# Two decoder layers on one core: the mean square behind three norms from three sums, taken ahead of the residual's update; order of the matmuls in some k-tiles

## The chip, the core and the metric

One core of a Trainium2 chip runs the whole program. The metric is the time of one execution on the device in microseconds (us); of three executions of the kernel before, the median is 2229.39 us.

## What is computed

The reference is two consecutive layers of a hybrid decoder trunk, 256 tokens of width 2048, all in float32. With shift, scale and gate rows from a projection of silu(c):

```
h  = RMSNorm(x) * (1 + scale_a) + shift_a
y  = concat(mLSTM(h @ W_in), attention(h @ W_in)) @ W_out
x  = x + gate_a * RMSNorm(y)
h' = RMSNorm(x) * (1 + scale_m) + shift_m
x  = x + gate_m * RMSNorm(relu(h' @ W_up)^2 @ W_down)
```

W_up is 2048 x 8192, W_down 8192 x 2048. RMSNorm divides by the root of the mean square over the 2048 columns and multiplies by a weight row. What matters here is the seam between two products: y is normed, added to x, and the sum is normed again before it can be multiplied by the next weight.

## The kernel before, in words

**Products.** Each float32 product is made of three products of rounded halves: a weight tile comes from HBM in loads of 1 MB (queue of SyncE, L231, six buffers called `raw`). ScalarE (ACT) copies half a load to the rounded `whi` (`split_hi`, L275), VectorE (DVE) subtracts it to get the rest `wlo` (`split_lo`, L285). Some pieces go into other buffers, with names like `hi_4h` (high half) and `hi_4l` (low half). Activations are split likewise (`hh`, `hl`, halves of a tile `ht`). A `Unit` is 512 output columns over all k-tiles; its matmuls on TensorE (PE) are at L389, or at L409 and L410 for wide units (`body_wide`: one matmul of 512 columns against `whi`, called W here, one of 256 against `wlo`, called n, for each of four column blocks of a k-tile: W n W n W n W n). One split feeds two k-tiles, called a slab. In layer 0 the rows of scale, shift and gate are still being made: `ada_op` (L244) streams 1 MB of weights through DVE, one instruction each.

**Seams.** Where a product ends and a norm leads to the next, `turn` (L587 to L660) writes the order out by hand: out-projection to up-projection of layer 0 (turn 1), down-projection of layer 0 to the in-projection of layer 1 (turn 2), out-projection to up-projection of layer 1 (turn 3). While it does so, every instruction is held in program order on its engine, and its line shows as L63. The 256 tokens are two tiles of 128 (token tile 0 and 1). The last unit of the old product runs token tile 0 first; while PE does token tile 1, ACT and DVE bring tile 0 through:

- `evac`: the square of y with its sum (ACT, `jko`, or `jkd` in turn 2), y times the gate row (DVE, `yg`; in turn 2 `ys`, last chunk `yl`), four chunks of 512 columns; only the last is within the turn, in turn 2 also the third of token tile 1 (`early`);
- `gain`: the four sums to r, one over the root (`rp..`, five small instructions on DVE and one on ACT);
- `update`: x = yg * r + x, four chunks (DVE);
- squares of the new x with their sums (ACT, `jkm`, or `jka`), then `root` (`rn..`), the same small chain;
- `scale`: x times that root for chunks 0 and 1 (`xn`, one on DVE, one on ACT);
- `group`: four transposes on PE (into `pst`), scale and shift (ACT, `hf`), rounding to `hh` (ACT), the rest `hl` (DVE).

Then the first matmuls of the new unit start with group 0 of tile 0, and tile 1 goes the same way; its group 0 is done by `group_fast`, in which DVE makes `hl` in two halves. The splits of the weights of the new unit (`split_hi`, `split_lo`) stand between these steps at written places. Chunks 2 and 3 follow outside the hand-written order (L62). After layer 1 the last norm updates x and stores it, with no second norm.

In the stages ahead of turns 1 and 3 (the out-projection, units `op_0` to `op_3` of 512 columns), `evac_out` (L1149) empties each unit; ahead of turn 2 `evac_down` (L1274) adds up the down-projection. A scheduler puts these among the splits by its own estimate.

Of the kernel before, what the change touches and what calls it, by code (L numbers as in the profile page):

```python
# [39 lines left out]
def hymba_kernel(ctx: ExitStack, tc: tile.TileContext, x_d, c_d, cols_d, cons_d, wada_d,  # L40
# [248 lines left out]
    def split():  # L289
        split_hi()  # L290
        split_lo()
# [48 lines left out]
    def xdone(n=1):  # L340
        live["x"] -= n
# [56 lines left out]
    def body_ws(u, xh, xl, wh, wl, kt):  # L398
        for j in range(4):
            cs = slice(j * P, (j + 1) * P)  # L400
            u.products(u.ps[j // 2][:, (j % 2) * S:(j % 2) * S + S], j // 2,
                       ((wh[:, cs], xh), (wh[:, cs], xl), (wl[:, cs], xh)), kt)

    def body_wide(u, xh, xl, wh, wl, kt):


        for j in range(4):
            cs = slice(j * P, (j + 1) * P)
            T.matmul(u.ps[j], wh[:, cs], u.act.both(kt), start=kt == 0, stop=False, skip_group_check=True)  # L409
            T.matmul(u.ps[j][:, 0:S], wl[:, cs], xh, start=False, stop=kt == u.nk - 1, skip_group_check=True)  # L410

    def body_mix(u, xh, xl, wh, wl, kt):
        for j in range(2):
# [28 lines left out]
    class PreNorm:  # L442


        def __init__(self, tag, l, vsc, vsh, yg=None, ssy=None):
            self.tag, self.l, self.vsc, self.vsh, self.yg, self.ssy = tag, l, vsc, vsh, yg, ssy
            self.xn, self.groups, self.r = {}, {}, {}

        def gain(self, tok):

# [4 lines left out]
        def update(self, tok, r, sq=None, store=False, between=None):  # L455

            for c in range(4):
                xc = x[:, tok, CH[c]]
                if r is not None:
                    V.scalar_tensor_tensor(xc, self.yg[c][tok], r, xc, ALU.mult, ALU.add)  # L460
                if between is not None and c == 3:
                    V.scalar_tensor_tensor(self.yg[c][tok], xc, 1.0, xc, ALU.mult, ALU.mult, accum_out=sq[:, c:c + 1])
                    between()
                elif sq is not None:
                    square_sum(xc, sq[:, c:c + 1], f"jk{self.tag}_{tok}_{c}")
                if store:
                    nc.sync.dma_start(out_d[tok, :, CH[c]], xc)
# [9 lines left out]
        def scale(self, tok, chunks):  # L477
            for c in chunks:
                o = self.xn[c, tok] = ytile(f"xn{self.tag}_{c}_{tok}")
                if c % 2:  # L480
                    A.activation(o, x[:, tok, CH[c]], AF.Copy, scale=self.r[tok])
                else:
                    V.tensor_scalar(o, x[:, tok, CH[c]], self.r[tok], None, ALU.mult)

        def norm(self, tok):
            sq = self.squares(tok)
            self.update(tok, None, sq)
            self.root(tok, sq)
            self.scale(tok, range(4))

        def group(self, g, tok):

            hh, hl, mods, hf = self.begin(g, tok)
            ps = xalloc(f"pst{self.tag}_{g}_{tok}")
            for k in range(4):
                T.transpose(ps[:, k * P:(k + 1) * P], self.xn[g, tok][:, k * P:(k + 1) * P], ident)
            for k, (gc, sc) in enumerate(mods):
                A.activation(hf[:, k, :], ps[:, k * P:(k + 1) * P], AF.Identity, bias=sc, scale=gc)
            xdone()
            A.activation(hh, hf, AF.Copy)  # L500
            return lambda: V.tensor_tensor(hl, hf, hh.bitcast(F32), ALU.subtract)
# [85 lines left out]
    def turn(units, evac, early, nrm, make, staged=None):  # L587

        s0 = st["mm"]
        units[0].slabs(1)
        split_to(s0 + 7)
        rest = []
        for i, u in enumerate(units[1:]):
            if early is not None and i == 3:
                early(0)
            side()  # L600
            rest.append((u, take()))
            u.mm(rest[-1][1], toks=(0,))
# [17 lines left out]
        units[-1].mm(rest[6][1], toks=(1,))  # L620
# [29 lines left out]
        strict["on"] = False  # L650
        for tok in range(2):
            nrm.scale(tok, range(2, 4))
        if staged:
            order, wide, small, done = staged
            xnT = {g: wide.tile([P, 4, S], F32, tag="sl", name=f"xnT{nrm.tag}_{g}") for g in (2, 3)}
            for tok in range(2):
                nrm.turn_in(xnT, tok, 2)
            strict["last"].clear()
            for m in make[1:]:
                units.append(m())  # L660
                units[-1].slabs(4)
            for e in range(4, 8):
                nrm.modulate(e, xnT, small)
                for u in order:
                    units[u].slabs(1)
                    if e == 7 and u < 3:
                        done(u, units[u])
            return units
        for g in (2, 3):
            for tok in range(2):  # L670
                nrm.group(g, tok)()
# [23 lines left out]
    for l in range(DEPTH):  # L695
# [449 lines left out]
        cT = lambda kt: (cg[kt // 4][0][:, kt % 4, :], cg[kt // 4][1][:, kt % 4, :])  # L1145
        yg = [[None, None] for _ in range(4)]
        ssy = smp.tile([P, 2, 4], F32, tag="ssy", name=f"ssy{L}")

        def evac_out(ps, c, tok):  # L1149
            yg[c][tok] = ytile(f"yg{L}_{c}_{tok}")  # L1150
            square_sum(ps[tok], ssy[:, tok, c:c + 1], f"jko{L}_{c}_{tok}")
            V.tensor_tensor(yg[c][tok], ps[tok], gps[l, GTA][:, CH[c]], ALU.mult)

        def evac_out_task(ps, c):
            for tok in range(2):
# [33 lines left out]
            t.finish()  # L1189


        hT2 = PreNorm("m" + L, l, SCM, SHM, yg, ssy)
        sT_ = {}
        ysum = [[None, None] for _ in range(4)]
        ssm_ = smp.tile([P, 2, 4], F32, tag="ssy", name=f"ssm_{L}")

        def s_tiles(u):
            sT_[u] = [sp.tile([P, 4, S], F32R, tag=f"s{a}", name=f"s{a}{L}_{u}") for a in "hl"]
# [73 lines left out]
        def evac_down(ps, e, c, tok):  # L1272
            if e == 0:
                ysum[c][tok] = ytile(f"ys{L}_{c}_{tok}")  # L1274
                A.activation(ysum[c][tok], ps[tok], AF.Copy)
                return
            yt = ysum[c][tok]
            V.tensor_tensor(yt, yt, ps[tok], ALU.add)
            if e == 7:
                square_sum(yt, ssm_[:, tok, c:c + 1], f"jkd{L}_{c}_{tok}")  # L1280
                o = yt
                if c == 3:
                    o = smp.tile([P, 4, P], F32, tag="hf", bufs=2, name=f"yl{L}_{tok}").rearrange("p a b -> p (a b)")
# [151 lines left out]
```

## Time and profile before

| | |
|---|---|
| times of the runs, us | 2231.54, 2229.39, 2228.36 |
| profiled execution, us | 2228.4 |
| its span in the profile, us | 2226.6 |
| busy share PE, DVE, ACT | 97%, 77%, 49% |
| mean granted TensorE clock | 0.988 |
| turn 1, 2, 3, us of the span | 406 to 440, 1132 to 1168, 1484 to 1519 |

The profiled execution is 1.8 us longer than its span (start and end), and 1.0 us shorter than the median. The profile gives a start and a duration for each instruction; matmuls overlap, so their pitch (from start to start) counts, not the duration. In a timeline row, the bracket is the idle time of the engine ahead of the instruction and what ended it; a row with "x4" is four alike, with one duration for all. The granted clock is the share of full speed that the throttle gave TensorE.

### The profile page before, as it was taken

To read this page: it belongs to the slowest core of one execution; us is meant where nothing else is said; L and a number is where in the kernel's file an instruction comes from. 1 tells how busy PE (TensorE), PEld (TensorE's weight loads), DVE (VectorE), ACT (ScalarE), POOL (GpSimd) and SP (SyncE) were. 2 spreads that over 40 slices of the span, in tenths; PEclk is the share of its full clock that TensorE was granted. 3 is DMA by queue.
4 is the path that set the end of the run, shared out by engine and by line. 5 is a ranking of instruction groups with operands and counts; after the bars stand their busy time and mean duration, and the time that the engine had idled before them with its cause. 6 is when DMAs were issued, how large, how long until landed. Compare 5 with 4: busy or idle time off the path is not lost.

```text
span 2226.6 us, 29814 instructions
## 1 busy us (share of the span) xinstructions
PE 2153.4 (97%) x11658; PEld 1836.8 (82%) x11658; DVE 1710.8 (77%) x2327; ACT 1102.1 (49%) x1597; POOL 1.4 (0%) x15
## 2 busy tenths in 40 slices
PE   6789999899999999999989999999999999999998
PEld 5779777798888888888879988778888888888886
DVE  7989999787888888888667898967566767555556
ACT  4246753645444444434555566556443444444434
POOL 0000000000000000000000000000000000000000
PEclk9999999999999999999999999999999999999999
DMA  9998679597889888888538866755666667655552
GB/s 380 390 366 301 238 301 350 199 355 306 305 318 343 295 337 315 316 319 313 202 131 328 314 229 245 263 191 196 236 223 233 228 225 265 209 189 189 189 189 76
DMA packets 82351, 589.88 MB, mean 265 GB/s; under 512 B 9185, under 2 KB 9633, under 8 KB 10785
## 3 DMA queue, kind: packets, MB, share of 16 engines
q1 hardware_dynamic: 82210, 587.98, 72.0%
q8 instruction: 91, 1.49, 0.3%
q14 instruction: 50, 0.41, 0.1%
HBM read 585.81 MB, written 2.13 MB: 264 GB/s over the span
## 4 chain that ended last, share of the span: by engine, by line
PE 85%; DVE 9%; ACT 3%; issue 2%; DMA 1%; SPq 0%; DVEq 0%; ACTq 0%
PE dn L389 31%; PE up L409 17%; PE up L410 9%; PE op L389 5%; PE up L389 5%; DVE raw L244 4%; PE om L389 3%; PE qa L389 2%; PE qm L389 2%; PE vm L389 2%; DVE wlo L285 2%; PE km L389 2%; PE kva L389 1%; PE up L63 1%; DVE x L63 1%
## 5 line engine op out<-in xcount | busy, mean ns | idle before, releaser
L285 DVE TENSOR_TENSOR wlo<-raw,whi 128x1024 fp32r<-128x1024 f32 x699 | 849.6, 1222 | 409.7 <-ACT whi L275 408.1
L275 ACT ACTIVATE whi<-raw 128x1024 fp32r<-128x1024 f32 x699 | 737.0, 1060 | 842.5 <-PE dn L389 338.7
L409 PE MATMUL up<-htm,whi 128*128 128x512 f32 x1664 | 588.2, 399 | 0.0
L410 PE MATMUL up<-htm,wlo 128*128 128x256 f32 x1664 | 466.9, 281 | 0.0
L244 DVE SCALAR_TENSOR_TENSOR raw<-raw,cact 128x2048 f32<-128x2048 f32 x192 | 437.3, 2284 | 8.2 <-DMA raw<-in_wada_dram 8.1
L389 PE MATMUL dn<-whi,sh 128*128 128x512 f32 x1004 | 391.3, 390 | 0.9 <-DVE r L1224 0.9
L389 PE MATMUL dn<-wlo,sh 128*128 128x512 f32 x1004 | 390.8, 389 | 0.0
L389 PE MATMUL dn<-whi,sl 128*128 128x512 f32 x1004 | 390.7, 389 | 0.0
L409 PEld LDWEIGHTS up<-htm,whi 128*128 128x128 f32 x1664 | 312.6, 188 | 77.6
L410 PEld LDWEIGHTS up<-htm,wlo 128*128 128x128 f32 x1664 | 314.2, 189 | 0.6
L389 PEld LDWEIGHTS dn<-whi,sh 128*128 128x128 f32 x1004 | 188.4, 188 | 41.0 <-DVE r L1224 1.4
L389 PEld LDWEIGHTS dn<-wlo,sh 128*128 128x128 f32 x1004 | 188.4, 188 | 39.6
L389 PEld LDWEIGHTS dn<-whi,sl 128*128 128x128 f32 x1004 | 188.5, 188 | 38.9 <-DVE sl L1246 0.2
L389 PE MATMUL op<-whi,ct 128*128 128x512 f32 x432 | 138.6, 400 | 2.6 <-ACT whi L275 1.8
L389 PEld LDWEIGHTS op<-whi,ct 128*128 128x128 f32 x432 | 81.6, 190 | 21.8 <-ACT whi L275 2.7
L389 PE MATMUL vm<-whi,hta 128*128 128x512 f32 x224 | 77.6, 429 | 21.1 <-ACT whi L275 18.5
L389 PE MATMUL qa<-hta,whi 128*128 128x256 f32 x512 | 93.7, 284 | 0.0
L389 PE MATMUL up<-htm,whi 128*128 128x256 f32 x512 | 93.0, 284 | 0.0
L389 PE MATMUL op<-wlo,ct 128*128 128x512 f32 x216 | 85.3, 401 | 3.0 <-DVE wlo L285 3.0
L389 PE MATMUL om<-whi,hta 128*128 128x512 f32 x256 | 82.2, 401 | 0.0
L389 PEld LDWEIGHTS up<-htm,whi 128*128 128x128 f32 x512 | 80.2, 192 | 0.5
L389 PEld LDWEIGHTS qa<-hta,whi 128*128 128x128 f32 x512 | 80.0, 192 | 0.7 <-issue 0.7
(388 smaller groups left out, 2435.7 us busy)
## 6 DMA issues: line engine op xcount, KB each, us to landing
raw<-in_wada_dram SPq DMA_DIRECT2D x192, 1024.0 KB, 6.3
raw<-in_wdn_dram SPq DMA_DIRECT2D x128, 1024.0 KB, 5.0
raw<-in_wup_dram SPq DMA_DIRECT2D x120, 1024.0 KB, 5.4
raw<-in_win_dram SPq DMA_DIRECT2D x56, 1024.0 KB, 5.3
raw<-in_wout_dram SPq DMA_DIRECT2D x32, 1024.0 KB, 6.6
raw<-in_wst_dram SPq DMA_DIRECT2D x16, 1024.0 KB, 7.6
raw<-in_wsu_dram SPq DMA_DIRECT2D x8, 1024.0 KB, 6.7
gp<-gdr SPq DMA_DIRECT2D x4, 1024.0 KB, 4.9
```

The costliest lines, as they stand in the source:

```text
L63: made = tc.keep_in_program_order(make(*args, **kw))
L244: V.scalar_tensor_tensor(w, w, 1.0, cact, ALU.mult, ALU.mult, accum_out=modc[l][:, v, j:j + 1])
L275: A.activation(hi, raw, AF.Copy)
L285: V.tensor_tensor(lo, raw, hi.bitcast(F32), ALU.subtract)
L389: T.matmul(o, a, w, start=not self.started[b], stop=last and i == 2, skip_group_check=True)
L409: T.matmul(u.ps[j], wh[:, cs], u.act.both(kt), start=kt == 0, stop=False, skip_group_check=True)
L410: T.matmul(u.ps[j][:, 0:S], wl[:, cs], xh, start=False, stop=kt == u.nk - 1, skip_group_check=True)
```

## The change

1. The mean square of the new x is no longer taken from the new x. As x' = x + r*y, sum(x'^2) = sum(x^2) + r * (sum(2xy) + r * sum(y^2)). The new `branch` follows every `yg` (in the out stages and, for the last slabs, the down stage of layer 0): DVE multiplies y, 2 and x with a sum, and writes the products, which nobody reads, over the emptied PSUM tile; ACT squares y with a sum (`jkb`). The new `old` squares the old x on ACT (`jkx`), two chunks with each of the first two `evac` steps of a token tile. `root_after` combines the sums with r in four small DVE instructions and takes the root, so the root comes ahead of the updates. For each of three turns that is eight more DVE instructions of 128x512 with a sum, of which one replaces an old square on DVE, and on ACT eight `jkb` and eight `jkx` in place of seven squares of the new x.
2. The turn then goes chunk by chunk: `step(0)`, `scale(0)`, `step(1)`, `scale(1)`, all on DVE; the steps of chunks 2 and 3 come later. The four parts of `group` are placed one by one.
3. The splits, the evacuation of tile 1 and `hl` stand at other places in the order; the transposes of group 1 of tile 1 go ahead of two runs of matmuls on PE.
4. In `body_wide` every eighth k-tile is ordered W W n n W W n n: 52 k-tiles of 26 units.

The queues of SyncE (all loads) and GpSimd have the same instructions in the same order.

```diff
     def body_wide(u, xh, xl, wh, wl, kt):
-        for j in range(4):
+        for j, wide in ONES if kt % 8 else TWOS:
...
+        def old(self, tok, c):
+            square_sum(x[:, tok, CH[c]], self.sums_of(tok)[:, 0, c:c + 1], f"jkx{self.tag}_{tok}_{c}")
+        def branch(self, tok, c, waste):
+            q, y = self.sums_of(tok), self.yg[c][tok]
+            V.scalar_tensor_tensor(waste, y, 2.0, x[:, tok, CH[c]], ALU.mult, ALU.mult, accum_out=q[:, 1, c:c + 1])
+            square_sum(y, q[:, 2, c:c + 1], f"jkb{self.tag}_{tok}_{c}")
...
+            V.tensor_reduce(q, self.sums[tok], AX.X, ALU.add)
+            V.tensor_scalar(v, q[:, 2:3], r, q[:, 1:2], ALU.mult, ALU.add)
+            V.scalar_tensor_tensor(v, v, r, q[:, 0:1], ALU.mult, ALU.add)
+            V.tensor_scalar(v, v, 0.0, 1.0 / D, ALU.max, ALU.mult)
+            self.r[tok] = rsqrt_one(v, 1, f"rn{self.tag}_{tok}")
...
         evac(0)
         r = nrm.gain(0)
         if not ahead:
             split_hi()
-        sq = nrm.squares(0)
-        nrm.update(0, r, sq)
-        if not ahead:
-            split_lo()
-        nrm.root(0, sq)
-        split_hi()
-        nrm.scale(0, range(2))
-        low = nrm.group(0, 0)
+        nrm.root_after(0, r)
+        nrm.step(0, 0, r)
+        nrm.scale(0, (0,), ())
+        nrm.step(1, 0, r)
+        nrm.scale(0, (1,), ())
+        steps = nrm.group(0, 0)
         units[-1].mm(rest[6][1], toks=(1,))
-        split_lo()
+        for f in steps[:3]:
+            f()
+        nrm.step(2, 0, r)
+        if not ahead:
+            split_lo()
+        split_hi()
         if early is not None:
             early(1)
+        steps[3]()
+        nrm.step(3, 0, r)
+        split_lo()
         evac(1)
-        low()
-        r = nrm.gain(1)
-        low = nrm.group(1, 0)
+        steps = nrm.group(1, 0)
...
-        sq = nrm.squares(1)
-        nrm.update(1, r, sq, between=low)
-        nrm.root(1, sq)
+        r = nrm.gain(1)
+        steps[0]()
+        nrm.root_after(1, r)
+        steps[1]()
+        steps[2]()
+        nrm.step(0, 1, r)
+        nrm.scale(1, (0,), ())
+        nrm.step(1, 1, r)
+        nrm.scale(1, (1,), ())
         split_hi()
-        nrm.scale(1, range(2))
-        nrm.group_fast(0, 1, split_lo)
+        steps[3]()
+        def between():
+            split_lo()
+            nrm.step(2, 1, r)
+        nrm.group_fast(0, 1, between)
         four.append(take())
         unit.mm(four[2], toks=(0,))
+        steps = nrm.group(1, 1)
         unit.mm(four[0], toks=(1,))
-        split()
-        low = nrm.group(1, 1)
         unit.mm(four[1], toks=(1,))
-        low()
+        split_hi()
+        for f in steps:
+            f()
+        split_lo()
+        nrm.step(3, 1, r)
         four.append(take())
...
             V.tensor_tensor(yg[c][tok], ps[tok], gps[l, GTA][:, CH[c]], ALU.mult)
+            hT2.branch(tok, c, ps[tok])
+            for k in ((0, 1), (2, 3), (), ())[c]:
+                hT2.old(tok, k)
```

What the scheduler and the written order make of this is seen in two places. First ACT near the end of `op_2`, the third unit of layer 0's out-projection, where `jko` needs PE's last matmul of `op_2`, and the first `whi` row below feeds the first matmuls of `op_3`. Before:

```order
L116 ACTIVATE jko_2_0_3591,ssy_2844<-op_2_0_3401 128x512
L116 ACTIVATE jko_2_1_3595,ssy_2844<-op_2_1_3402 128x512
L275 ACTIVATE whi_3531<-raw_3463 128x1024
L275 ACTIVATE hi_0h<-raw_3463 128x1024
L1255 ACT_TABLE_LOAD
```

And after the change, at the same place:

```order
L116 ACTIVATE jkxm_1_3_3461,sumsm_1_3257<-x 128x512
L275 ACTIVATE whi_3551<-raw_3380 128x1024
L275 ACTIVATE whi_3561<-raw_3493 128x1024
L275 ACTIVATE hi_0h<-raw_3493 128x1024
L116 ACTIVATE jko_2_0_3621,ssy_2844<-op_2_0_3417 128x512
L275 ACTIVATE hi_1h<-raw_3495 128x1024
```

The first two splits for `op_3` (`whi_3531` before, `whi_3561` after, and `hi_0h`) stood behind the evacuation of `op_2` and now stand ahead of it.

Second DVE in turn 1, token tile 1, from the root to the subtraction `hi_5l` that PE needs for its second slab; `htm_1` is the `hl` of group 1 of token tile 0. Before:

```order
L63 TENSOR_TENSOR htm_1_3789<-hfm_1_0_3790,htm_1_3789 128x4x128
L63 TENSOR_REDUCE ssqm_1_3828<-sqm_1_3815 128x1
L63 TENSOR_SCALAR rnm_1_v<-ssqm_1_3828 128x1
L63 RECIPROCAL rnm_1_y<-rnm_1_y 128x1
L63 TENSOR_SCALAR rnm_1_t<-rnm_1_y,rnm_1_v 128x1
L63 SCALAR_TENSOR_TENSOR rnm_1_y<-rnm_1_t,rnm_1_y 128x1
L63 TENSOR_SCALAR xnm_0_1_3843<-x,rnm_1_y 128x512
L63 TENSOR_TENSOR hi_5l<-raw_3529,hi_5h 128x1024
```

And after the change:

```order
L63 TENSOR_SCALAR rnm_1_t<-rnm_1_y,rnm_1_v 128x1
L63 SCALAR_TENSOR_TENSOR rnm_1_y<-rnm_1_t,rnm_1_y 128x1
L63 SCALAR_TENSOR_TENSOR x<-yg_0_1_3253,rpm_1_y,x 128x512
L63 TENSOR_SCALAR xnm_0_1_3867<-x,rnm_1_y 128x512
L63 SCALAR_TENSOR_TENSOR x<-yg_1_1_3452,rpm_1_y,x 128x512
L63 TENSOR_SCALAR xnm_1_1_3870<-x,rnm_1_y 128x512
L63 TENSOR_TENSOR htm_1_3816<-hfm_1_0_3817,htm_1_3816 128x4x128
L63 TENSOR_TENSOR hi_5l<-raw_3559,hi_5h 128x1024
L63 SCALAR_TENSOR_TENSOR x<-yg_2_1_3627,rpm_1_y,x 128x512
```

Between `xnm_0_1`, which lets PE do the transposes, and `hi_5l` there was nothing; now an update, a scale and the `hl` of group 1 stand there.

More of the change, by code (lines that the diff above doesn't have):

```diff
@@ L402, in body_ws @@
                        ((wh[:, cs], xh), (wh[:, cs], xl), (wl[:, cs], xh)), kt)
+    ONES = [(j, w) for j in range(4) for w in (1, 0)]
+    TWOS = [(j + k, w) for j in (0, 2) for w in (1, 0) for k in range(2)]
     def body_wide(u, xh, xl, wh, wl, kt):
-        for j in range(4):
+        for j, wide in ONES if kt % 8 else TWOS:
             cs = slice(j * P, (j + 1) * P)
-            T.matmul(u.ps[j], wh[:, cs], u.act.both(kt), start=kt == 0, stop=False, skip_group_check=True)
-            T.matmul(u.ps[j][:, 0:S], wl[:, cs], xh, start=False, stop=kt == u.nk - 1, skip_group_check=True)
+            if wide:
+                T.matmul(u.ps[j], wh[:, cs], u.act.both(kt), start=kt == 0, stop=False, skip_group_check=True)
+            else:
+                T.matmul(u.ps[j][:, 0:S], wl[:, cs], xh, start=False, stop=kt == u.nk - 1, skip_group_check=True)
     def body_mix(u, xh, xl, wh, wl, kt):
@@ L446, in __init__ @@
             self.tag, self.l, self.vsc, self.vsh, self.yg, self.ssy = tag, l, vsc, vsh, yg, ssy
-            self.xn, self.groups, self.r = {}, {}, {}
+            self.xn, self.groups, self.r, self.sums = {}, {}, {}, {}
         def gain(self, tok):
@@ L453, in gain, with sums_of, step @@
             return rsqrt_one(tot, D, f"rp{self.tag}_{tok}")
[L455 to L467, printed above, removed]
+        def sums_of(self, tok):
+            if tok not in self.sums:
+                self.sums[tok] = smp.tile([P, 3, 4], F32, tag="sums", name=f"sums{self.tag}_{tok}")
+            return self.sums[tok]
+        def old(self, tok, c):
[4 more added lines that the diff above has]
+            square_sum(y, q[:, 2, c:c + 1], f"jkb{self.tag}_{tok}_{c}")
+        def step(self, c, tok, r, store=False):
+            xc = x[:, tok, CH[c]]
+            V.scalar_tensor_tensor(xc, self.yg[c][tok], r, xc, ALU.mult, ALU.add)
+            if store:
+                nc.sync.dma_start(out_d[tok, :, CH[c]], xc)
         def squares(self, tok):
@@ L475, in root, with root_after, scale @@
             self.r[tok] = rsqrt_one(ssq, D, f"rn{self.tag}_{tok}")
-        def scale(self, tok, chunks):
+        def root_after(self, tok, r):
+            q = smp.tile([P, 3], F32, tag="sums3", name=f"sum3{self.tag}_{tok}")
+            v = smp.tile([P, 1], F32, tag="ssq1", name=f"ssq{self.tag}_{tok}")
+            V.tensor_reduce(q, self.sums[tok], AX.X, ALU.add)
[3 more added lines that the diff above has]
+            self.r[tok] = rsqrt_one(v, 1, f"rn{self.tag}_{tok}")
+        def scale(self, tok, chunks, by=(1, 3)):
             for c in chunks:
                 o = self.xn[c, tok] = ytile(f"xn{self.tag}_{c}_{tok}")
-                if c % 2:
+                if c in by:
                     A.activation(o, x[:, tok, CH[c]], AF.Copy, scale=self.r[tok])
@@ L486, in norm @@
             sq = self.squares(tok)
-            self.update(tok, None, sq)
+            for c in range(4):
+                square_sum(x[:, tok, CH[c]], sq[:, c:c + 1], f"jk{self.tag}_{tok}_{c}")
             self.root(tok, sq)
@@ L496, in group, with scaled, whole_group @@
                 T.transpose(ps[:, k * P:(k + 1) * P], self.xn[g, tok][:, k * P:(k + 1) * P], ident)
[L497 to L501, printed above, removed]
+            def scaled(ks):
+                for k in ks:
+                    A.activation(hf[:, k, :], ps[:, k * P:(k + 1) * P], AF.Identity, bias=mods[k][1], scale=mods[k][0])
+                if 3 in ks:
+                    xdone()
+            return (lambda: scaled((0, 1)), lambda: scaled((2, 3)), lambda: A.activation(hh, hf, AF.Copy),
+                    lambda: V.tensor_tensor(hl, hf, hh.bitcast(F32), ALU.subtract))
+        def whole_group(self, g, tok):
+            for f in self.group(g, tok):
+                f()
         def group_fast(self, g, tok, between):
@@ L611, in turn @@
             split_hi()
-        sq = nrm.squares(0)
-        nrm.update(0, r, sq)
+        nrm.root_after(0, r)
[4 more added lines that the diff above has]
+        steps = nrm.group(0, 0)
+        units[-1].mm(rest[6][1], toks=(1,))
+        for f in steps[:3]:
+            f()
+        nrm.step(2, 0, r)
         if not ahead:
             split_lo()
-        nrm.root(0, sq)
         split_hi()
-        nrm.scale(0, range(2))
-        low = nrm.group(0, 0)
-        units[-1].mm(rest[6][1], toks=(1,))
-        split_lo()
         if early is not None:
             early(1)
+        steps[3]()
+        nrm.step(3, 0, r)
+        split_lo()
         evac(1)
-        low()
-        r = nrm.gain(1)
-        low = nrm.group(1, 0)
+        steps = nrm.group(1, 0)
         unit = make[0]()
@@ L631, in turn @@
             unit.mm(slab, toks=(0,))
-        sq = nrm.squares(1)
-        nrm.update(1, r, sq, between=low)
-        nrm.root(1, sq)
-        split_hi()
-        nrm.scale(1, range(2))
-        nrm.group_fast(0, 1, split_lo)
+        r = nrm.gain(1)
[7 more added lines that the diff above has]
+        nrm.scale(1, (1,), ())
+        split_hi()
+        steps[3]()
[3 more added lines that the diff above has]
+        nrm.group_fast(0, 1, between)
         four.append(take())
         unit.mm(four[2], toks=(0,))
+        steps = nrm.group(1, 1)
         unit.mm(four[0], toks=(1,))
-        split()
-        low = nrm.group(1, 1)
         unit.mm(four[1], toks=(1,))
-        low()
+        split_hi()
+        for f in steps:
+            f()
+        split_lo()
+        nrm.step(3, 1, r)
         four.append(take())
@@ L650, in turn @@
         strict["on"] = False
+        hold["hi"], hold["lo"], hold["ada"] = [strict["last"][e] for e in (A, V, V)]
         for tok in range(2):
@@ L670, in turn @@
             for tok in range(2):
-                nrm.group(g, tok)()
+                nrm.whole_group(g, tok)
         strict["last"].clear()
@@ L1147, in hymba_kernel @@
         ssy = smp.tile([P, 2, 4], F32, tag="ssy", name=f"ssy{L}")
+        hT2 = PreNorm("m" + L, l, SCM, SHM, yg, ssy)
         def evac_out(ps, c, tok):
@@ L1189, in hymba_kernel @@
             t.finish()
-        hT2 = PreNorm("m" + L, l, SCM, SHM, yg, ssy)
         sT_ = {}
@@ L1195, in hymba_kernel @@
         ssm_ = smp.tile([P, 2, 4], F32, tag="ssy", name=f"ssm_{L}")
+        nxt = PreNorm(f"a{l + 1}", l + 1, SCA, SHA, ysum, ssm_) if l + 1 < DEPTH else PreNorm("f", l, 0, 0, ysum, ssm_)
         def s_tiles(u):
@@ L1285, in evac_down @@
                 ysum[c][tok] = o
+                if l + 1 < DEPTH:
+                    nxt.branch(tok, c, ps[tok])
+                    for k in ((0, 1), (2, 3), (), ())[c]:
+                        nxt.old(tok, k)
         def evac_down_task(un, e, c):
@@ L1333, in hymba_kernel @@
         if l + 1 < DEPTH:
-            hT = PreNorm(f"a{l + 1}", l + 1, SCA, SHA, ysum, ssm_)
-            starts = turn([previous] * 4 + [un] * 4, evac_last, lambda tok: evac_down(previous.ps, 7, 2, tok), hT,
+            hT = nxt
+            starts = turn([previous] * 4 + [un] * 4, evac_last, lambda *a: evac_down(previous.ps, 7, 2, *a), hT,
                           [lambda: Unit(f"vm0{l + 1}", ("in", l + 1, UV0), KT, hT, body_xs),
@@ L1338, in hymba_kernel @@
         else:
-            fin = PreNorm("f", l, 0, 0, ysum, ssm_)
             un.slabs_by_token()
@@ L1343, in hymba_kernel @@
                 evac_last(tok)
-                fin.update(tok, fin.gain(tok), store=True)
+                r = nxt.gain(tok)
+                for c in range(4):
+                    nxt.step(c, tok, r, store=True)
             strict["on"] = False
```

## The prediction

> **What bounds the kernel now.** I read the page first: shares of the engines, then the chain that ended last.
>
> ```profile
> span 2226.6 us, 29814 instructions
> PE 2153.4 (97%) x11658; PEld 1836.8 (82%) x11658; DVE 1710.8 (77%) x2327; ACT 1102.1 (49%) x1597; POOL 1.4 (0%) x15
> PE 85%; DVE 9%; ACT 3%; issue 2%; DMA 1%; SPq 0%; DVEq 0%; ACTq 0%
> ```
>
> PE is the bound; DVE holds the chain for 9%. The profiled execution took 2228.4 us (1.8 over the span), 1.0 under the median 2229.39; I sum on 2228.4 and add 1.0. The windows by stage show where PE is not full (columns: window, length, busy PE, PEld, DVE, ACT, POOL, granted clock, DMA share, GB/s).
>
> ```profile
> 406.00:440.00 34.00, 29.17 (x129) 22.72 (x128) 25.34 (x54) 25.41 (x54) 0.00 (x0) 0.90 0.33 123
> 1132.00:1168.00 36.00, 29.61 (x134) 23.07 (x133) 26.82 (x57) 25.67 (x57) 0.20 (x2) 0.91 0.26 90
> 1484.00:1519.00 35.00, 28.79 (x135) 23.21 (x134) 25.57 (x53) 26.22 (x56) 0.00 (x0) 0.90 0.25 91
> 340.00:388.00 48.00, 44.95 (x192) 34.64 (x191) 47.35 (x61) 17.07 (x24) 0.00 (x0) 1.00 0.92 359
> 388.00:406.00 18.00, 16.22 (x64) 12.59 (x63) 11.17 (x13) 10.45 (x14) 0.00 (x0) 0.91 0.96 362
> 520.00:1130.00 610.00, 609.08 (x3030) 514.33 (x3029) 497.49 (x558) 275.84 (x322) 0.00 (x0) 1.00 0.82 304
> ```
>
> Between the turns PE is full. The three turns idle 4.8, 6.4 and 6.2 us, and run at a clock of 0.90; the out-projection of layer 0 ahead of turn 1 idles too, and there DVE is the full engine (47.35 of 48). PE's own waits, from its timeline: turn 1 (token 0's transposes, its `hl`, token 1's transposes), turn 2 and turn 3.
>
> ```profile
> 415.20 0.66 PE L63 MATMUL pstm<-cons,xnm 128*128 128x128 f32 x4 [0.19 <-DVE xnm L63]
> 420.02 0.74 PE L63 MATMUL up<-hi_3h,htm 128*128 128x512 f32 x2 [1.17 <-DVE htm L63]
> 426.94 0.63 PE L63 MATMUL pstm<-cons,xnm 128*128 128x128 f32 x4 [2.90 <-DVE xnm L63]
> 1146.95 0.73 PE L63 MATMUL vm<-hi_h,hta 128*128 128x512 f32 x2 [2.53 <-DVE hta L63]
> 1153.78 0.66 PE L63 MATMUL psta<-cons,xna 128*128 128x128 f32 x4 [2.91 <-DVE xna L63]
> 1154.91 0.79 PE L63 MATMUL vm<-wlo,hta 128*128 128x512 f32 x1 [0.25 <-DVE wlo L63]
> 1504.67 1.09 PE L63 MATMUL pstm<-cons,xnm 128*128 128x128 f32 x4 [4.36 <-DVE xnm L63]
> ```
>
> Token 0's root, which the change shortens most, costs PE 0.19 us. The costly waits are token 0's `hl` and token 1's transposes. DVE in turn 1, with one row (1145.60) of turn 2:
>
> ```profile
> 409.50 2.74 DVE L63 SCALAR_TENSOR_TENSOR x<-yg,rpm_y,x 128x512 f32<-128x512 f32 x4
> ...
> 414.66 0.49 DVE L63 TENSOR_SCALAR xnm<-x,rnm_y 128x512 f32<-128x512 f32 x1
> ...
> 418.68 0.69 DVE L63 TENSOR_TENSOR yg<-op,gp 128x512 f32<-128x512 f32 x1 [2.40 <-ACT jko L63]
> 419.29 0.68 DVE L63 TENSOR_TENSOR htm<-hfm,htm 128x512 fp32r<-128x512 f32 x1
> ...
> 423.87 0.69 DVE L63 SCALAR_TENSOR_TENSOR yg<-x 128x512 f32<-128x512 f32 x1
> ...
> 425.09 0.15 DVE L63 TENSOR_REDUCE ssqm<-sqm 128x1 f32<-128x4 f32 x1
> ...
> 426.30 0.49 DVE L63 TENSOR_SCALAR xnm<-x,rnm_y 128x512 f32<-128x512 f32 x1
> 426.70 1.22 DVE L63 TENSOR_TENSOR hi_5l<-raw,hi_5h 128x1024 fp32r<-128x1024 f32 x1
> ...
> 1145.60 0.69 DVE L63 TENSOR_TENSOR yl<-ys,gp 128x512 f32<-128x512 f32 x1
> ```
>
> **Turn 1, token 0.** r is there at 409.50 in both. Four small combining steps at about 0.2 (five in 1.21 from 425.09 to 426.30), that root's 1.2, one update 0.69 and one scale 0.49 end near 412.6; now the scale ends at 415.15. That is 2.5 us sooner, but PE was busy until 415.01 with the token-1 matmuls that stand ahead of the transposes, so the gain is the wait of 0.19. The `hl` at 419.29 stands behind `yg`, which waited for ACT's `jko`; now it stands ahead of `yg`, starts when `hh` is there (about 417.9) and ends near 418.5, where PE arrives at 418.85 less 0.2. So the 1.17 falls to about 0.2: a gain of 1.0.
>
> **Turn 1, token 1.** What was moved comes back here. Ahead of `yg` now stand `hl` (0.6), the update of chunk 3 (0.6) and the subtraction of `hi_4` (1.14), which itself waits on ACT behind `hh`. The subtraction, done beforehand until now, ends near 420.4, and PE stops for it some 0.5. `yg` starts near 420.35 instead of 418.68. Then: `yg` 0.6, the cross sum 0.7 (price of 423.87, the nearest instruction with a sum; it writes PSUM, which no row shows, so 0.6 to 0.9), r 1.2, combining 0.8, root 1.1, update 0.6 to 0.7: `xnm` at 425.4 against 426.30, a chain of 5.05 instead of 7.62. The transposes come 0.9 sooner, not 2.5. PE's idle time ahead of them grows in one piece to about 4, since the `hl` wait ahead is gone. Next PE needs `hi_5l`. Now it follows `xnm` at once (426.70, done 427.92). Then an update (0.65), a scale (0.4) and `hl` (0.6), which needs ACT's `hh`, stand between: start near 427.0, end 428.2, and PE, at about 426.1, waits some 2.1 where it waited under 0.3. That takes back 1.8. Two later splits (ACT's first for the next unit behind the group 1 work, DVE's for the fourth slab) add 0.3 to 0.4 each; part hides in the half-speed stretch. Turn 1: -0.9 + 1.8 + 0.3 = **+1.2** (0.3 to 1.9).
>
> **Turn 3** has the same order without the stage of layer 0 ahead: the same walk gives -0.8 and +1.8, and the two late splits 0.6 where no half-speed stretch hides them: **+1.6** (0.3 to 1.9).
>
> **Turn 2.** Here `early` puts the third chunk of token 1, with its cross sum, ahead of token 0's `hl`, and on ACT a `whi` copy (1.05, row 391.43 below) now stands ahead of that chunk's `jkd`, for which the in-place gate product waits. `hl` is no sooner, and the wait of 2.53 stays. `yl` (1145.60) moves behind the cross sum, `hl`, an update and a split, to about 1149.0: 3.4 later. The chain from it to `xna` is about 5.3 instead of 7.6; the transposes come 0.5 to 1.1 later. Then the `wlo` at 1154.91 (0.25) waits about 2.1, as in turn 1; the next unit's first `whi`, on ACT behind group 1, up to 1.1 more, hidden if PE runs at half speed. 1.1 + 1.8 = **+2.9** (1.5 to 4.4).
>
> **The out-projection of layer 0.** Rows of PE, then of ACT:
>
> ```profile
> 362.74 0.73 PE L389 MATMUL op<-wlo,ct 128*128 128x512 f32 x2 [0.33 <-DVE wlo L285]
> ...
> 380.44 0.74 PE L389 MATMUL op<-wlo,ct 128*128 128x512 f32 x2 [0.65 <-DVE wlo L285]
> ...
> 392.53 1.30 PE L389 MATMUL op<-whi,ct 128*128 128x512 f32 x4 [1.78 <-ACT whi L275]
> ...
> 394.81 1.05 PE L389 MATMUL op<-whi,ct 128*128 128x512 f32 x2
> ```
>
> ```profile
> 390.11 0.60 ACT L116 ACTIVATE jko<-op 128x512 bf16<-128x512 f32 x1 [10.16 <-PE op L389]
> ...
> 391.43 1.05 ACT L275 ACTIVATE whi<-raw 128x1024 fp32r<-128x1024 f32 x1
> ```
>
> PE waits for DVE's `wlo` already. Now `yg` of tile 1 and a cross sum stand in front of the one for 362.74 (+1.3), and two cross sums of `op_1` in front of the one for 380.44 (+1.4, two of 0.7): 2.7 later. `op_2`'s fall into DVE's free time (11.17 of 18 busy). On the other side the first split of `op_3` no longer stands behind `jko`: the wait of 1.78 at 392.53 goes, and with it about 1.2 of half-speed matmuls behind it (pairs of 1.05 at 394.81 against 0.73 at 362.74). A late `wlo` for the last slab adds some 0.3. 2.7 - 1.8 - 1.2 + 0.3 = 0, taken as **+0.2** (-1.7 if the loads, at a share of 0.96, hide part of the delay; +2.9 if the split is late all the same).
>
> The same work ahead of turns 2 and 3 I put at nothing: six cross sums (4.2) and fourteen ACT squares meet engines with 497.49 and 275.84 busy of 610. If that cover went, it would cost up to 4 each. SP and POOL queues do not move. The last norm does the same steps: 0.
>
> **The wide k-tiles.** Eight pairs W n, first and ninth W:
>
> ```profile
> 899.92 0.40 PE L409 MATMUL up<-htm,whi 128*128 128x512 f32 x1
> ...
> 902.74 0.40 PE L409 MATMUL up<-htm,whi 128*128 128x512 f32 x1
> ```
>
> 0.353 a pair. The change makes 104 groups of two pairs, of which half the transitions become like to like. Like to like for 512 columns is shown in the down-projection, 18 steps from here to here:
>
> ```profile
> 559.73 0.39 PE L389 MATMUL dn<-whi,sh 128*128 128x512 f32 x1
> ...
> 563.81 0.39 PE L389 MATMUL dn<-whi,sh 128*128 128x512 f32 x1
> ```
>
> 0.227 each; with half of that for 256 columns, a group at best costs 0.69 against 0.705, 0.6 to 1.3 in all. I take **-0.6** (-1.3 to 0).
>
> **Sum.** 0.2 + 1.2 + 2.9 + 1.6 - 0.6 = +5.3: 2233.7 on the profiled execution, **2234.7** beside the median.
>
> **The rivals.** *A, faster.* The chain is 2.5 shorter for each token, and nothing takes its place: PE's waits for token 1 shrink by that and `hl`'s by 1.0. That is 3.5 in turns 1 and 3; in turn 2, with `yl` 3.4 later, nothing; with the 1.7 that one half-speed window costs in each of the two, -10: about 2219. For it: all three waits at the transposes hang on that chain. Against it: 426.70 follows 426.30 now, and three instructions come between. It decides by whether `hi_5l` is done before PE has finished with its first half slab. Chance 0.18. *B, no change.* The two late splits and the wait for `hi_5l` lie in stretches that PE runs at half speed anyway, so that half of the 5.7 in the turns goes: about 2232. Chance 0.17. *C, clearly slower by the clock.* The idle pieces of about 4 in turns 1 and 3 and two of 2 to 3 in turn 2 each bring one half-speed window more than now. How such a window looks now:
>
> ```profile
> 420.00:425.00 5.00, 4.01 (x10) 2.65 (x10) 4.65 (x12) 4.38 (x12) 0.00 (x0) 0.66 0.06 25
> ```
>
> A clock of 0.66 over 5 us is 1.7 lost to a full-speed PE; three more are +5: 2239.8. Against it: the rows have such windows in every turn at 0.90 already, behind waits of only 1 to 3. Chance 0.10. The Trainium skill, page "TensorE: Matmul & The Clock Gate", section "Why this matters for your kernels", advises no idle gap over about 3 us, since one idle window sends the clock back to half: by that rule the waits of 2.90 are harmless and those of 4 are not, which is C. The trace shows half speed behind shorter gaps, 1.17 at 420.02 among them, so by the trace the change adds little. That the root comes sooner and PE cannot use it for token 0 is part of the forecast.
>
> **How the numbers follow.** My forecast has 0.55. A measurement tells 0.2% (4.5 us) from no change: 2224.9 to 2233.8 is the same. The forecast's own range, all low and all high ends, is -0.9 to +11.1: 2228.5 to 2240.5; I put 0.15 of its 0.55 under 2233.8. Faster 0.18 (A); the same 0.17 + 0.15 = 0.32; slower 0.40 + 0.10 = 0.50. The range goes from 2225, a third of the way from the own range to A, up to 2241, which takes in C.
>
> **What would show it.** Right: PE's wait at token 0's `hl` in turns 1 and 3 under 0.4; transposes of token 1 about 1 us sooner there, and a new wait of about 2 for `hi_5l` right behind; in turn 2 `yl` 3 us later; no wait at the start of `op_3`, but waits of 1 to 2 for `wlo` in `op_1` and `op_2`. Wrong: `hi_5l` without a wait, turns shorter than 34, 36 and 35 us, or cross sums far from 0.7.

## The result

The changed kernel takes 2242.55 us (2242.03 to 2244.16) against 2228.88 for the kernel before: the ratio is 1.0062, with a 95% interval of 1.0044 to 1.0079. It is slower by 13.7 us. The forecast was 2234.7 with a range up to 2241: right in sign, but the time lies beyond the range, and the 13.7 are more than twice the 5.3 of the sum.

### The profile after

The first lines of the page of the changed kernel:

```profile
span 2240.7 us, 29902 instructions
PE 2163.7 (97%) x11658; PEld 1836.4 (82%) x11658; DVE 1732.1 (77%) x2393; ACT 1115.4 (50%) x1645; POOL 1.4 (0%) x15
```

PE is as full as before, but has 10.3 us more busy time for the same 11,658 matmuls. So a good part of the loss isn't in waits at all. Windows of 42 us, laid wholly into wide units of the up-projection and wholly into a stretch of the down-projection, show where. The number in brackets behind PE's busy time is how many matmuls started. Of before:

```profile
897.00:939.00 42.00, 42.00 (x239) 36.46 (x238) 34.08 (x41) 18.05 (x21) 0.00 (x0) 1.00 0.88 320
943.00:985.00 42.00, 42.00 (x187) 34.76 (x186) 37.19 (x44) 17.47 (x19) 0.00 (x0) 1.00 0.87 321
```

Of after:

```profile
902.00:944.00 42.00, 42.00 (x245) 36.72 (x244) 33.99 (x41) 18.56 (x22) 0.00 (x0) 1.00 0.87 323
947.00:989.00 42.00, 42.00 (x182) 34.03 (x182) 36.55 (x45) 17.10 (x18) 0.00 (x0) 1.00 0.86 314
```

In both, PE is busy all the time at the full granted clock. The wide units got through 245 matmuls instead of 239, the down-projection through only 182 instead of 187. The mean step from start to start says the same: in the wide units a pair W n takes 347.6 ns instead of 353.1, in the down-projection a matmul takes 232.4 instead of 227.0. With 1664 pairs and 3012 matmuls that is some 9.2 us gained and some 16.3 lost. Neither is in my prediction, but for 0.6 of the gain.

The waits in the turns look much as forecast. PE's waits of after, of turn 1, turn 2 and turn 3:

```profile
417.34 0.50 PE L63 MATMUL up<-hi_3h,htm 128*128 128x512 f32 x1 [0.43 <-ACT htm L63]
419.87 0.50 PE L63 MATMUL up<-hi_4l,htm 128*128 128x512 f32 x1 [0.38 <-DVE hi_4l L63]
425.43 1.09 PE L63 MATMUL pstm<-cons,xnm 128*128 128x128 f32 x4 [4.12 <-DVE xnm L63]
428.33 0.79 PE L63 MATMUL up<-hi_5l,htm 128*128 128x512 f32 x1 [1.39 <-DVE hi_5l L63]
...
1152.54 1.22 PE L63 MATMUL vm<-hi_h,hta 128*128 128x512 f32 x2 [2.89 <-DVE hta L63]
1160.55 1.12 PE L63 MATMUL psta<-cons,xna 128*128 128x128 f32 x4 [3.38 <-DVE xna L63]
1163.47 0.79 PE L63 MATMUL vm<-wlo,hta 128*128 128x512 f32 x1 [1.38 <-DVE wlo L63]
...
1512.92 1.09 PE L63 MATMUL pstm<-cons,xnm 128*128 128x128 f32 x4 [4.14 <-DVE xnm L63]
1515.82 0.80 PE L63 MATMUL up<-hi_5l,htm 128*128 128x512 f32 x1 [1.38 <-DVE hi_5l L63]
```

Token 0's wait for `hl` (1.17 in turns 1 and 3) is gone. The wait at token 1's transposes is one piece of 4.1 in turns 1 and 3, and of 3.4 in turn 2. Behind it stands the new wait for `hi_5l`, and in turn 2 for a `wlo`, of 1.4. DVE in turn 1 of after, token 1:

```profile
419.73 0.69 DVE L63 TENSOR_TENSOR yg<-op,gp 128x512 f32<-128x512 f32 x1
420.45 0.70 DVE L63 SCALAR_TENSOR_TENSOR op<-yg,x 128x512 f32<-128x512 f32 x1
421.07 0.14 DVE L63 DVE_READ_ACCUMULATOR op<-yg,x 128x1 f32 x1
...
424.80 0.49 DVE L63 TENSOR_SCALAR xnm<-x,rnm_y 128x512 f32<-128x512 f32 x1
...
427.06 1.22 DVE L63 TENSOR_TENSOR hi_5l<-raw,hi_5h 128x1024 fp32r<-128x1024 f32 x1
```

From `yg` to `xnm` it is 5.07 us (5.05 in the prediction), the cross sum costs 0.70 as priced, and `hi_5l` starts at 427.06 (427.0). In turn 2 the in-place gate product indeed waits for ACT's `jkd`, and `yl` comes at 1154.91. Counted from the turn's first `jkd` (1133.15 before, 1138.68 after) that is 3.8 later than before; the forecast was 3.4:

```profile
1150.46 0.69 DVE L63 TENSOR_TENSOR ys<-ys,gp 128x512 f32<-128x512 f32 x1 [3.82 <-ACT jkd L63]
...
1154.91 0.69 DVE L63 TENSOR_TENSOR yl<-ys,gp 128x512 f32<-128x512 f32 x1
```

### The profile page after: what moved, and what is told of

Read it like the earlier page. It is cut to its first block, busy times and chain, and to the rows that moved or that the text cites. A ratio compares the mean times of both kernels' runs of the same rounds, so it can differ in the third digit from the quotient of the medians.

```text
span 2240.7 us, 29902 instructions
## 1 busy us (share of the span) xinstructions
PE 2163.7 (97%) x11658; PEld 1836.4 (82%) x11658; DVE 1732.1 (77%) x2393; ACT 1115.4 (50%) x1645; POOL 1.4 (0%) x15
## 4 chain that ended last, share of the span: by engine, by line
PE 87%; DVE 8%; ACT 3%; issue 1%; DMA 1%; SPq 0%; DVEq 0%; ACTq 0%
PE dn L389 31%; PE up L414 17%; PE up L416 8%; PE op L389 6%; PE up L389 5%; DVE raw L244 4%; PE om L389 3%; PE qa L389 2%; PE vm L389 2%; PE qm L389 2%; DVE wlo L285 2%; PE km L389 2%; PE kva L389 1%; PE up L63 1%; PE op L63 1%
## 5 line engine op out<-in xcount | busy, mean ns | idle before, releaser
L414 PE MATMUL up<-htm,whi 128*128 128x512 f32 x1664 | 571.9, 394 | 0.0
L416 PE MATMUL up<-htm,wlo 128*128 128x256 f32 x1664 | 444.7, 277 | 0.0
L389 PE MATMUL dn<-whi,sh 128*128 128x512 f32 x1004 | 396.5, 395 | 1.1 <-DVE r L1282 1.1
L389 PE MATMUL dn<-whi,sl 128*128 128x512 f32 x1004 | 396.2, 395 | 0.0
L389 PE MATMUL dn<-wlo,sh 128*128 128x512 f32 x1004 | 396.2, 395 | 0.0
L414 PEld LDWEIGHTS up<-htm,whi 128*128 128x128 f32 x1664 | 305.9, 188 | 64.5
L389 PEld LDWEIGHTS up<-htm,whi 128*128 128x128 f32 x512 | 80.0, 192 | 1.0 <-ACT whi L275 0.6
```

Of the source, the lines that this page charges most:

```text
L389: T.matmul(o, a, w, start=not self.started[b], stop=last and i == 2, skip_group_check=True)
```

## The experiments

My theory after the result, A: the turns cost what the sum says, and two things in the long stages explain the rest. The order W W n n makes all wide matmuls faster, not only those in the reordered k-tiles. And the down-projection is slower because its activations lie elsewhere: the new small tiles `sums` (48 bytes, rounded to 64) and `sums3` (32), four buffers each, take 4 x 64 + 4 x 32 = 384 bytes of a pool that lies ahead of them. In the memory map of the compiled program (which says at which byte of each partition a tile lies) `sh` moves from byte 194048 to 194432; `whi`, `wlo` and the `ht` tiles stay. The kernel before has an unused tile `page` of 640 bytes (L1165) just ahead of `sh`. The rival, B: the paces follow from something else, the order of the work or busier engines beside PE.

### Each of the two alone, and each undone

e1 is the kernel before with the new `body_wide` alone:

```diff
-        for j in range(4):
+        for j, wide in ONES if kt % 8 else TWOS:
```

> The kernel before, with only the new order of every eighth k-tile (W W n n). Theory A (this order alone speeds up all wide matmuls, from 353 to 347 ns a pair W n over 1664 pairs): 9.3 us faster, about 2219.6, the down-projection's pitch stays 227 ns. Theory B (the wide pitch changed for another reason, such as where tiles lie): pairs stay at 353 ns, time within 1 us of before. My forecast's term was -0.6 us.

Measured: 2217.71 against 2230.01, ratio 0.9947 (0.9932 to 0.9962). Windows as above, wide units and down-projection:

```profile
892.00:934.00 42.00, 42.00 (x244) 36.73 (x243) 34.49 (x41) 18.57 (x22) 0.00 (x0) 1.00 0.88 324
936.00:978.00 42.00, 42.00 (x187) 34.77 (x186) 37.28 (x47) 18.15 (x19) 0.00 (x0) 1.00 0.88 327
```

A pair takes 347.7 ns, and the down-projection stays at 226.9. One k-tile in eight was reordered and nearly all pairs became faster: A. This kernel beats both of the two. Of its 12.3 us, the pace explains some 9. In the profiled executions 2.2 us stand already at the first `jko` of the out-projection, and 1.5 more come from the out-projection itself.

e2 is the kernel before with `page` enlarged, so that `sh` and `sl` lie as in the changed kernel:

```diff
-.tile([P, 160], F32, name=f"page{L}")
+.tile([P, 256], F32, name=f"page{L}")
```

> The kernel before, with only the unused tile ahead of the MLP's tiles made 384 bytes larger, so that the activations sh and sl of the down-projection lie 384 bytes later in each partition, as in the changed kernel. Theory A (their place sets the pitch of the down-projection's matmuls): pitch 232.4 instead of 227.0 ns over 3012 matmuls, 16.3 us slower, about 2245. Theory B (the slower pitch came from the order of work or from busier engines): no change, 2229.

Measured: 2241.3, ratio 1.0052 (1.0035 to 1.0069). Two windows in wide units and one in the down-projection:

```profile
722.00:764.00 42.00, 42.00 (x240) 36.39 (x239) 31.66 (x36) 17.83 (x22) 0.00 (x0) 1.00 0.83 305
812.00:854.00 42.00, 42.00 (x245) 36.72 (x244) 33.22 (x39) 18.23 (x22) 0.00 (x0) 1.00 0.84 315
856.00:898.00 42.00, 42.00 (x182) 34.04 (x182) 35.70 (x40) 17.67 (x19) 0.00 (x0) 1.00 0.82 297
```

Not an instruction differs from before but for addresses, and the down-projection falls to 232.6 ns: A. A few other tiles that lie behind `page` move with `sh` and `sl`; but for 18 of its matmuls, the down-projection reads only `sh` and `sl` of them. The loss is 11.3, not 16.3, and the first two rows say why: with the old order of the wide matmuls some units run at the slow pace (240 in 42 us, 354 ns a pair) and some at the fast one (245, 347 ns), 349.7 on the mean, which gives back 5.7. In the kernel before, all but the first unit were slow. Here neither the order of the wide matmuls nor the place of what they read (`htm`, `whi`, `wlo`) has changed, so the order is not all that sets their pace.

e3 is the changed kernel with `page` made smaller, so that `sh` is back at 194048:

```diff
-.tile([P, 160], F32, name=f"page{L}")
+.tile([P, 64], F32, name=f"page{L}")
```

> The changed kernel, with the unused tile made 384 bytes smaller, so that sh and sl lie where they lay before. Theory A: down-projection back at 227.0 ns, 16.3 us faster than the changed kernel, about 2226. Theory B: stays at 2242.6. The turns themselves (new waits, half-speed windows) stay about 5 us slower than before in both.

Measured: 2224.08, ratio to before 0.9977 (0.9967 to 0.9987). The stretch of the down-projection:

```profile
939.00:981.00 42.00, 42.00 (x187) 34.80 (x186) 37.73 (x47) 17.93 (x19) 0.00 (x0) 1.00 0.89 325
```

Back at 187 and 226.9 ns; 18.5 us faster than the changed kernel. With the address mended, the change as a whole would have been faster than before, by its wide matmuls.

e4 is the changed kernel with the old order in all wide k-tiles (`in ONES`).

> The changed kernel, with the old order W n in all wide k-tiles. Theory A: wide pairs back at 353 ns, 9.3 us slower than the changed kernel, about 2252. Theory B: wide pairs stay at 347 ns, time within 1 us of 2242.6.

Measured: 2247.0, ratio 1.0077 (1.0062 to 1.0092), 4.5 us over the changed kernel, half of what A expected. The reason is that of e2: the pairs take 350.0 on the mean, with the same units fast and slow as in e2, but for the first unit, which is slow here.

### Which addresses are slow

Theory X: rows of 512 bytes must start at a multiple of 512. Theory Y: the distance to the streamed weights counts. Four kernels are e1 with `page` larger by 128, 256, 512 and 2048 bytes.

> The kernel before with the new order of every eighth k-tile, and the down-projection's activations sh and sl 128 bytes later. Theory X (their 512-byte rows must start at a multiple of 512 bytes): pitch of the down-projection 232.5 ns, span some 16 us over the same kernel without the shift (2214.6). Theory Y (what counts is their distance to the weights that are streamed, in steps far larger than 512 bytes, and 384 happened to be bad): a small shift changes nothing, 227 ns.

> As the last, 256 bytes later. Theory X: 232.5 ns. Theory Y: 227 ns, or a pitch that goes up with the shift (228 to 231) if the loss grows with the part of the row that lies over the boundary.

> As the last, 512 bytes later, again at a multiple of 512 (and of 2048). Theory X: 227 ns, span within 2 us of 2214.6. Theory Y: past the bad distance or within it, 232 ns or more.

> As the last, 2048 bytes later, a multiple of 512. Theory X: 227 ns, span within 2 us of 2214.6. Theory Y: 232 ns possible.

Measured, in one execution each: spans of 2234.9, 2220.3, 2218.0 and 2219.7 us. The down-projection with 128 bytes more:

```profile
946.00:988.00 42.00, 42.00 (x183) 34.05 (x182) 36.21 (x44) 17.65 (x19) 0.00 (x0) 1.00 0.88 315
```

And with 256 bytes more:

```profile
942.00:984.00 42.00, 42.00 (x187) 34.77 (x186) 37.16 (x45) 17.86 (x19) 0.00 (x0) 1.00 0.88 330
```

Shifts of 0, 256, 512 and 2048 give 226.8 to 226.9 ns, shifts of 128 and 384 give 232.4 and 232.6. X is wrong in its size, Y altogether: in these six placements what counts is whether the rows start at a multiple of 256 bytes (194048 is 758 x 256, and 194432 lies in the middle between two). The address matters for `sh` and `sl`, which these matmuls load as weights of the array; no run moved the streamed operand.

### Is one reordered k-tile a unit enough?

e12 is e1 with W W n n in the first k-tile of each wide unit alone (`in ONES if kt else TWOS`).

> The kernel before with the order W W n n in the first k-tile of each wide unit alone (26 instead of 52 k-tiles). Theory S (a unit runs wholly at one of two paces, and the new order sets the fast one, which then stays): all units at 347 ns a pair, 2217.7 as with every eighth k-tile. Theory L (the gain lies in the reordered k-tiles and those near them): about half of the gain, 2223.

Measured: 2221.8, ratio 0.9969 (0.9956 to 0.9982). A window in wide units:

```profile
895.00:937.00 42.00, 42.00 (x245) 36.72 (x244) 34.62 (x41) 18.58 (x22) 0.00 (x0) 1.00 0.89 326
```

Pairs take 347.6 ns on the mean, with 26 reordered k-tiles as with 52: S by the pace, though not for every unit. Three stretches stay slow: the first unit from its third k-tile, the first unit of layer 1 from its second, and one unit of layer 1 from 1904 to its end, behind a small matmul of another kind (`psg`, at 1903.65) that comes between its own. Two rows of the second, 16 pairs apart, give 353.8 ns:

```profile
1550.57 0.40 PE L413 MATMUL up<-htm,whi 128*128 128x512 f32 x1
...
1556.23 0.40 PE L413 MATMUL up<-htm,whi 128*128 128x512 f32 x1
```

In e1 the same three stretches are slow, although W W n n comes again in their ninth k-tile; in the changed kernel it does make the first unit fast from there. In all, 369 of the 416 wide k-tiles run below 350 ns a pair in e1 and in e12, and 14 in the kernel before.

The time of 2221.8 lies nearer to L's 2223 than to S's 2217.7, and the interval overlaps with e1's. The profiled executions differ by 2.8 us, but 3.0 stand already at the first `jko` (351.04 against 348.02), ahead of the first wide unit; so L isn't borne out. A wide unit runs at one of two paces and mostly keeps it, and W W n n at its start brings the faster one in nearly all units. Why it does, no run here shows.

### What the turns cost, and whether a better order mends it

e3 and e1 have the same paces in the long stages and differ in the three sums and the turns: 2224.08 - 2217.71 = 6.4 us. Of the 6.6 between their profiled executions, 2.1 stand already at the first `jko` (350.16 against 348.02). Turn 2 in e1, from token 0's last `jkd` to the first copy of the new unit's result:

```profile
1125.64 0.63 ACT L63 ACTIVATE jkd<-ys 128x512 bf16<-128x512 f32 x1 [4.71 <-DVE ys L63]
...
1181.79 0.60 ACT L992 ACTIVATE va<-vm 128x512 f32<-128x512 f32 x1 [1.20 <-PE vm L389]
```

And in e3:

```profile
1128.37 0.63 ACT L63 ACTIVATE jkd<-ys 128x512 bf16<-128x512 f32 x1 [1.36 <-DVE ys L63]
...
1187.69 0.60 ACT L1041 ACTIVATE va<-vm 128x512 f32<-128x512 f32 x1 [1.20 <-PE vm L389]
```

56.15 against 59.32: 3.2 us. The same way, from token 0's `jko` in the turn to the first copy of the new unit's result (`r`), turn 1 takes 104.1 in e1 and 105.4 in e3, and turn 3 55.4 and 56.4: they cost 1.3 and 1.0. Is that the price of the order that I blamed? e9 is e3 with the subtraction ahead of group 1's `hl` again; e10 is e3 with token 0's `hl` ahead of `early`; e11 has both.

```diff
         split_hi()
+        split_lo()
         steps[3]()
-
-        def between():
-            split_lo()
-            nrm.step(2, 1, r)
-
-        nrm.group_fast(0, 1, between)
+        nrm.group_fast(0, 1, lambda: nrm.step(2, 1, r))
...
+        steps[3]()
         if early is not None:
             early(1)
-        steps[3]()
```

The part above the dots is e9's, the part below is e10's.

> The changed kernel with sh and sl back in their old place (2224.1), and in each turn the subtraction that PE waits for behind token 1's transposes (hi_5l in turns 1 and 3, the wlo in turn 2) put ahead of the hl of group 1 again. Theory P (the waits of 1.39, 1.38 and 1.39 there are paid in full): they go, 4 us faster and one half-speed window less, 2218.5 to 2220.5. Theory Q (DVE's chain behind them is late anyway, so the wait moves to the next hl): within 1 us of 2224.

> The changed kernel with sh and sl back in their old place (2224.1), and in turn 2 token 0's hl ahead of the third chunk of token 1 (only turn 2 has that chunk). Theory P: the wait of 2.89 for hl falls to about 0.3, token 1's chain starts 0.6 later, so the wait at its transposes grows by what was gained: within 1 us of 2224, unless a half-speed window goes. Theory R (the stretch of four half-speed windows in turn 2 hangs on that first wait): the stretch falls from 13.7 to 6.8 us, 3 us faster, 2221.

> Both edits together. Theory P: as the first, 2218.5 to 2220.5. Theory R: 2 to 3 us better still, about 2217.

Measured: 2223.4 (0.9976, 0.9966 to 0.9985), 2224.75 (0.9983, 0.9974 to 0.9993) and 2223.85 (0.9977, 0.9968 to 0.9986), all the same as e3. The 4 us that P expected don't come. But the edit of e9 doesn't take the wait away either: the wait for `hi_5l`, or the `wlo` in turn 2, shrinks only by 0.3 to 0.6, and turn 2 runs no shorter at half speed (17.1 us against 13.7):

```profile
428.14 0.79 PE L63 MATMUL up<-hi_5l,htm 128*128 128x512 f32 x1 [1.07 <-DVE hi_5l L63]
...
1506.04 0.80 PE L63 MATMUL up<-hi_5l,htm 128*128 128x512 f32 x1 [0.78 <-DVE hi_5l L63]
```

DVE in turn 1 of e9 shows why:

```profile
425.62 0.74 DVE L63 SCALAR_TENSOR_TENSOR x<-yg,rpm_y,x 128x512 f32<-128x512 f32 x1
426.47 0.48 DVE L63 TENSOR_SCALAR xnm<-x,rnm_y 128x512 f32<-128x512 f32 x1
426.87 1.22 DVE L63 TENSOR_TENSOR hi_5l<-raw,hi_5h 128x1024 fp32r<-128x1024 f32 x1
```

Only the `hl` (0.6) has gone behind `hi_5l`. The update and the scale of chunk 1 (1.25 together) still stand ahead of it, and it starts as soon as they are done. By the same stretches as above, the turns of e9 are 0.3, 0.65 and 0.3 shorter than those of e3, about as much as the waits shrank. That is too little for the medians to show, and it speaks for waits that are paid; a run without the wait isn't among these.

In e10 the wait for `hl` moves to the next operand, the `wlo` (2.89 and 0.29 become one of 3.19), and the half-speed stretch of 13.7 stays, so R is refuted too:

```profile
1143.89 0.79 PE L63 MATMUL vm<-wlo,hta 128*128 128x512 f32 x1 [3.19 <-DVE wlo L63]
```

## Why the prediction failed, point by point

- **The wide k-tiles, -0.6 (-1.3 to 0).** This step failed. It priced the transitions in the 104 reordered groups and held all others fixed. The pace of nearly all units changed as a whole: -9.2 us by the pace, and e1 as a whole -12.3 (0.9932 to 0.9962, or 8.5 to 15.2 us).
- **The term that was missing.** The prediction counted instructions and queues, but the change also adds tiles, and they move `sh` and `sl` by 384 bytes: +16.3 us by the pace, shown by e2, e3 and e5. The unused tile `page` in the kernel before stood there to be asked about. These two failures together are +7.7 (16.3 - 9.2 + 0.6) and put the result outside the range; with e3 in place of the changed kernel the sign would have been the other.
- **Turn 1, +1.2.** Right in mechanism and about in size (1.3 between e1 and e3): the gain of 0.9 at the transposes, the `hi_4l` wait (0.38, forecast 0.5) and the new wait for `hi_5l`, 1.39, where I had 2.1. How much of the loss that wait alone is stays open: e9 shortens it by 0.3 and the turn by as much.
- **Turn 3, +1.6.** 1.0, within its bounds of 0.3 to 1.9.
- **Turn 2, +2.9.** 3.2. The `hl` wait stayed (2.89, forecast 2.5), `yl` came late by the `jkd`, as said. I had not seen how long PE would then run at half speed, 13.7 us in e3 against 6.8 in e1, so it is in part luck that the sum of the waits comes near the measured loss. Between the profiled executions of before and after, where turns 2 and 3 also have more half-speed windows, the three turns differ by 1.8, 3.9 and 1.4, in all 7.1.
- **The out-projection of layer 0, +0.2.** From the first `jko` to the first of the turn it takes 56.65 before:

```profile
350.24 0.60 ACT L116 ACTIVATE jko<-op 128x512 bf16<-128x512 f32 x1 [2.24 <-PE op L389]
...
406.89 0.60 ACT L63 ACTIVATE jko<-op 128x512 bf16<-128x512 f32 x1 [6.25 <-PE op L389]
```

and 55.00 after:

```profile
351.45 0.60 ACT L116 ACTIVATE jko<-op 128x512 bf16<-128x512 f32 x1 [2.20 <-PE op L389]
...
406.45 0.60 ACT L63 ACTIVATE jko<-op 128x512 bf16<-128x512 f32 x1 [3.24 <-PE op L389]
```

  That is 1.65 sooner, at the low end of the bounds (-1.7). The wait of 1.78 at the start of `op_3` is gone, as forecast. Of the two waits for `wlo` that were to grow, the first did, from 0.33 to 1.78:

```profile
365.44 0.73 PE L389 MATMUL op<-wlo,ct 128*128 128x512 f32 x2 [1.78 <-DVE wlo L285]
```

  The second (0.65 at 380.44 before, to grow by 1.4) is gone instead; this term failed, and the forecast counted it in full. The half-speed window, too, didn't go but came earlier. e1, in the old order, takes 55.12 and has no half-speed window there, and e3, in the new order, 54.75 without one; so most of the difference of before goes with that window, which before falls at 393.47 and after at 366.84. With this, the paces, the 7.1 of the turns and 1.2 that stand already at the first `jko`, 13.8 of the 14.1 us between the two profiled executions are placed.
- **The rivals.** A was wrong, as the waits did come. B was wrong too: waits do lie in half-speed stretches, but the turns cost 5.5 between e1 and e3, and not half of 5.7. C came true in turn 2 (five half-speed windows instead of two) and by one window in turn 3 (three instead of two; e3 has two there), and not in turn 1 (two in both). Half speed in turn 2 lasted from 1152 to 1169:

```profile
1152.00:1169.00 17.00, 11.71 (x30) 8.63 (x31) 13.39 (x33) 9.52 (x23) 0.20 (x2) 0.50 0.18 62
```

  Before, the windows there were two of 3.4 us with a full one between:

```profile
1147.82:1151.23 3.41, 3.04 (x8) 1.84 (x6) 3.33 (x6) 3.31 (x9) 0.20 (x2) 0.50 0.00 0
1151.23:1154.64 3.41, 0.86 (x5) 0.58 (x5) 3.10 (x10) 2.48 (x7) 0.00 (x0) 1.00 0.00 0
```

  So after, PE was not given full speed again after a half-speed window in which it had idled by 0.6 of 3.4 us (it began at 1152.54), while before it was after one with 0.4 of idle time (3.41 - 3.04). The Trainium skill, page "TensorE: Matmul & The Clock Gate", section "What's actually happening", says that full speed returns after a window that is busy throughout. The trace agrees as far as all half-speed windows without idle time were followed by full speed, but the window at 1147.82 shows that a little idle time did no harm. Over the fourteen traces, but for their first 20 us, half-speed windows with up to 0.23 us of PE idle were all followed by full speed (121), those with 0.58 or more all by half speed (65), and between the two both occur. The same way, full-speed windows with up to 1.59 us of idle, in however many pieces, were all followed by full speed, and those with 1.84 or more all by half speed. My range took C in at 2239.8, but not on top of the rest.

What stays open: why a wide unit picks one pace or the other, and why an odd multiple of 128 bytes costs 5.5 ns a matmul. The first 350 us also varied by up to 5.0 us between the profiled executions (the first `jko` at 348.02 in e1 and at 353.01 in e6), and no run here says why.

## What to carry to other kernels

Where PE is the bound, read the pace of its matmuls, by their number in equal windows of each stage, before the waits; half a per cent of 2,200 us hides in steps of 5 ns. Compare the memory maps as well as the instruction orders of two kernels: a few small tiles in an early pool can move the operands of a whole stage. And a shorter chain ahead of one wait pays only if what the next wait hangs on moves up with it (here the subtraction `hi_5l`, behind an update, a scale and an `hl`).

## What the runs showed of the hardware that was not expected

- Matmuls of 512 columns in fp32r whose loaded weights lie at multiples of 256 bytes in the partition step at 227 ns, those at 128 bytes beside them at 232.4 to 232.6 (ten kernels and four).
- A stream of alternating matmuls of 512 and 256 columns runs at 347 or at 354 ns a pair for a whole stretch of up to 256 matmuls (two units), at the same granted clock of 1.00 and with the same tiles. Two like ones after each other once, at the start of each unit, brought 369 of 416 k-tiles to 347, where 14 were before.
- At half speed, a window of 3.4 us with 0.6 of idle time in it was followed by another at half speed, five in a row in turn 2. At full speed, 1.84 us of idle time within a window, in several pieces, was always enough to bring half speed.
